# The TensorE work of a mixture-of-experts stage put into one written order, in a kernel that runs a chain of network blocks

## The chip, the core and the metric

The kernel runs on one core of one Trainium2 chip. The metric is the device time of one execution in microseconds (us). All arrays are float32 in HBM. TensorE (PE in the rows) multiplies, VectorE (DVE) and ScalarE (ACT) do the element work, GpSimd (POOL) a little of it, and SyncE (SP) issues nearly all loads.

## The reference, cut to what matters

The network is a chain of blocks on 256 tokens of width 1024. The part at issue is the feed-forward of the first block, a mixture of 32 experts of which each token takes 4:

```python
def expert_block(args):
    xb, e = args
    u = xb @ w_mlp1[e] + b_mlp1[e]                     # 1024 -> 2048
    x_glu = jnp.minimum(u[..., ::2], SWIGLU_LIMIT)
    x_lin = jnp.clip(u[..., 1::2], -SWIGLU_LIMIT, SWIGLU_LIMIT)
    a = x_glu * jax.nn.sigmoid(SWIGLU_ALPHA * x_glu) * (x_lin + 1)
    return a @ w_mlp2[e] + b_mlp2[e]                   # 1024 -> 1024
...
out = jnp.zeros((T + 1, D), jnp.float32).at[slot_tok].add(ys.astype(jnp.float32) * slot_gate[:, None])
```

One expert has 8 MiB of first weights and 4 MiB of second weights, so the 32 experts have 384 MiB, and each of them is read once.

## The kernel before

`moe` (L1944) takes the 32 experts in 16 pairs, `for p in range(16)` (L1980). The tokens of the two experts of a pair share the 128 columns that TensorE holds: 64 and 64 slots, or 96 and 32 slots in the four pairs after the first ("wide" pairs, `WIDE`). A product with a slice of 64 (or 32) slots uses only that part of the array, so products of different slices can run side by side.

The weights come as 384 loads of 1 MiB (`chunks`, L2057): for each pair 16 for the first product (8 steps of 128 rows, one load for each expert) and 8 for the second (4 double steps). They go round through 14 buffers of 1 MiB, nine of the pool `wm` and five of the pool `wp` (`chunk`, L2052). SyncE issues a load when its buffer has been read for the last time.

A pair has these parts, in the order in which the program writes them:

- `slots(p+1)`: VectorE writes the one-hot matrices `S` and `SG` of the next pair.
- `bias` (L2034): b_mlp1 added to the four accumulators `u` by products with one-hot rows, 8 instructions. In the first pair it follows `up`, in the others it goes ahead.
- `up` (L2154): 64 products of 128x512 (128 in a wide pair), for each step k, each quarter n, each expert.
- `hidden` (L2168): the activation, on VectorE and ScalarE, quarter by quarter, into `a`.
- `take` (L1873): 16 products for each half b of the tokens gather the next pair's tokens into two accumulators `taken`; `inputs` (L2141) copies them to `X`, four copies on VectorE and four on ScalarE.
- `give` (L2217): 4 products add the results of the previous pair to the output `y`.
- `shares` (L2180): two transposes of `SG`. `turned` (L2189): 8 transposes of `a`, copied to `aT` by ScalarE in two halves.
- `bias` with b_mlp2, 4 instructions, then `down` (L2199): 32 products of 128x512 (64 in a wide pair).
- `results` (L2211): ScalarE copies the two accumulators to `ye`.

The order that the program writes is not the order in which TensorE runs. A planner that knows the dependencies and has its own costs and due times orders each engine's instructions when the program is built, so products of one part may stand between those of another. `issue_after(ins)` binds an instruction to come behind another one on its engine. It adds no wait on a semaphore. Before the change only the loads of the first pair (`dma`, L127, `self.queue`) and the first pair's bias are bound so.

Accumulators of 128x512 lie in PSUM: four banks for `acc()` (the four of `u`) and four for `gps()`, which `taken`, `o`, the transposes and `give` share. A float32 product of 512 columns is two matmul records in the trace.

Of the kernel before, what the change touches and what calls it, by code (L numbers as in the profile page):

```python
# [18 lines left out]
P = 128  # L19
# [19 lines left out]
class Net:  # L39
    def __init__(self, ctx, tc, dram, cols):  # L40
        self.ctx, self.tc, self.nc, self.d, self.colat = ctx, tc, tc.nc, dram, cols
        self.n, self.normed, self.later, self.queue = 0, (), None, None
        e = ctx.enter_context
        self.cp = e(tc.tile_pool(name="cp", bufs=1))
        self.xp = e(tc.tile_pool(name="xp", bufs=1))
        self.sp = e(tc.tile_pool(name="sp", bufs=4))
        self.wp = e(tc.tile_pool(name="wp", bufs=5))
        self.psa = e(tc.tile_pool(name="psa", bufs=4, space=PSUM))
        self.psg = e(tc.tile_pool(name="psg", bufs=4, space=PSUM))
        self.cols = self.const("c_cols")  # L50
        self.ident = self.const("c_ident")
        self.mhalf = self.cp.tile([P, 1], F32, name="mhalf", tag="mhalf")
        self.nc.vector.memset(self.mhalf, -0.5)
        self.x = self.xp.tile([P, 2, D], F32, name="x", tag="x")
# [1818 lines left out]
    def take(self, banks, S, m, b):  # L1873

        for k in range(8):
            j = k % 4
            self.nc.tensor.matmul(  # L1877
                banks[k // 4][:, j * m : (j + 1) * m], self.x[:, b, k * P : (k + 1) * P], S[:, b, :m],
                start=b == 0 and j == 0, stop=b == 1 and j == 3,
            )  # L1880
# [63 lines left out]
    def moe(self, ctx, A2, B2, ahead):  # L1944


        nc, d = self.nc, self.d
        self.wm = self.pool(ctx, "wm", self.WM)
        self.turn = 0
        mp = self.pool(ctx, "moe")  # L1950
        y = self.tl(mp, [P, 2, D], "ymoe")
        bias = self.biases(mp)
        self.queue = []
        nc.gpsimd.memset(y, 0.0)
        hot4 = self.tl(mp, [P, 32], "id4")
        nc.vector.tensor_reduce(hot4, self.ident.rearrange("p (r e) -> p e r", r=4), axis=AX.X, op=ALU.add)
        QG, perm, ei = (self.Q, self.G), hot4, None

        def slots(p):

            wide = 0 < p <= self.WIDE
            S = self.tl(mp, [P, 2, P], "S", bufs=2) if p else None
            SG = self.tl(mp, [P, 2, P], "SG", bufs=2)
            hs = self.tl(mp, [P, P], "hot", F32R, bufs=2)
            ws, at = [], 0
            for h, n in enumerate((96, 32) if wide else (64, 64)):
                c = 2 * p + h
                q, g = ([QG[i][:, b, c : c + 1] for b in range(2)] for i in range(2))
                self.chosen(q, g, n, at, S, SG)
                nc.gpsimd.tensor_copy(hs[:, at : at + n], perm[:, c : c + 1].to_broadcast([P, n]))  # L1970

                step = 32 if wide else 64
                ws.append((c, [slice(i, i + step) for i in range(at, at + n, step)]))
                at += n
            return S, SG, hs, ws

        with self.tc.high_priority():
            X = self.inputs(mp, self.taken, P, A2, B2)
        now, give = slots(0), None
        for p in range(16):  # L1980
            _, SG, hs, ws = now
            w = [(d["w_mlp1"][c], d["w_mlp2"][c]) if p == 0 else self.weights(self.expert(ei[0:1, c : c + 1])) for c, _ in ws]
            loads = self.chunks([(*wc, sls) for wc, (_, sls) in zip(w, ws)], self.chunk)
            if p == 0:
                qg, perm, cnt, ei = self.pairs(mp)
                QG = qg[:, 0], qg[:, 1]
            if p < 15:
                now = slots(p + 1)
            u = [self.acc() for _ in range(4)]
            begin = lambda: self.bias(u, bias[0], hs, P, p > 0, p == 0)  # L1990
            last = self.up(u, X, loads, None if p == 0 else begin)
            if p == 0:
                with self.tc.issue_after(last):
                    begin()
            a = self.hidden(mp, u, P)
            if p < 15:
                taken = [self.gps() for _ in range(2)]
                for b in range(2):
                    self.take(taken, now[0], P, b)
                X = self.inputs(mp, taken, P, A2, B2)  # L2000
            if give:
                give()
            sT = self.shares(mp, SG, P)
            aT = self.turned(mp, a, P)
            o = [self.gps() for _ in range(2)]
            self.bias(o, bias[1], hs, P, True, False)
            self.down(o, aT, loads)
            if p == 15:
                ahead()
            give = self.results(mp, o, sT, y, P)  # L2010
            if p == 0:
                self.queue = None
                self.ada_row(self.g2)
                items = self.overflow_items(mp, cnt)
        give()
        with self.tc.issue_after(self.split_v):
            n = nc.values_load(
                items[0][0:1, 0:1], min_val=0, max_val=self.ITEMS, skip_runtime_bounds_check_because="computed on the chip"
            )
        self.overflow(mp, QG, ei, A2, B2, y, n, items)  # L2020
        return y
# [12 lines left out]
    def bias(self, banks, b, hot, m, first, last):  # L2034

        parts = (b.h, b.l)
        for j, part in enumerate(parts):
            for n, bank in enumerate(banks):
                r = slice(32 * n, 32 * n + 32)
                self.nc.tensor.matmul(  # L2040
                    bank[:m, :], hot[r, :m], part[r, :], start=first and j == 0, stop=last and j == len(parts) - 1
                )

    def expert(self, v, engines=(mybir.EngineType.SP,)):
        return self.nc.values_load(
# [57 lines left out]
    def overflow(self, mp, QG, ei, A2, B2, y, n, items):  # L2103
        nc, d = self.nc, self.d
        _, ci, bf = items
        with self.tc.For_i(0, n, 1) as i:
# [23 lines left out]
                self.take(taken, S, 64, b)  # L2130
            X = self.inputs(mp, taken, 64, A2, B2)
            u = [self.acc() for _ in range(4)]
            self.up(u, X, loads, lambda: begin(u, b1))
            sT = self.shares(mp, SG, 64)
            aT = self.turned(mp, self.hidden(mp, u, 64), 64)
            o = [self.gps() for _ in range(2)]
            begin(o, b2)
            self.down(o, aT, loads)
            self.results(mp, o, sT, y, 64)()

    def inputs(self, mp, taken, m, A2, B2):  # L2141
# [9 lines left out]
                    self.ts(X[:, k, :m], src, A2[:, k : k + 1], ALU.mult, B2[:, k : k + 1], ALU.add)  # L2151
        return X

    def up(self, u, X, loads, begin=None):  # L2154

        if begin:
            begin()
        for k in range(8):
            raws = next(loads)
            for n in range(4):  # L2160
                for raw, sl in raws:
                    last = self.nc.tensor.matmul(  # L2162
                        u[n][sl, :], X[:, k, sl], raw[:, n * 512 : (n + 1) * 512],
                        start=k == 0 and not begin, stop=k == 7 and bool(begin),
                    ).ins
        return last

    def hidden(self, mp, u, m):  # L2168
        a = self.tl(mp, [P, D], "a")
# [10 lines left out]
    def shares(self, mp, SG, m):  # L2180

        sT = self.tl(mp, [P, 2, P], "sT", bufs=2)
        ps = self.gps()
        for b in range(2):
            self.nc.tensor.transpose(ps[:m, b * P : (b + 1) * P], SG[:, b, :m], self.ident)
        self.nc.vector.tensor_copy(sT[:m], ps[:m, :T].rearrange("p (b t) -> p b t", b=2))
        return sT

    def turned(self, mp, a, m):  # L2189
        aT = self.tl(mp, [P, 8, P], "aT")  # L2190
        for q in range(2):
            ps = self.gps()
            for j in range(4):
                k = 4 * q + j
                self.nc.tensor.transpose(ps[:, j * m : (j + 1) * m], a[:m, k * P : (k + 1) * P], self.ident[:m, :m])
            self.nc.scalar.copy(aT[:, 4 * q : 4 * q + 4, :m], ps[:, : 4 * m].rearrange("p (k s) -> p k s", s=m))
        return aT

    def down(self, o, aT, loads):  # L2199

        for k in range(0, 8, 2):
            raws = next(loads)
            for f in range(2):
                for n in range(2):
                    for raw, sl in raws:
                        self.nc.tensor.matmul(  # L2206
                            o[n][sl, :], aT[:, k + f, sl], raw[:, f * D + n * 512 : f * D + (n + 1) * 512],
                            start=False, stop=k + f == 7,
                        )

    def results(self, mp, o, sT, y, m):  # L2211

        ye = self.tl(mp, [P, D], "ye")
# [3 lines left out]
        def give():  # L2217
            for b in range(2):
                for n in range(2):
                    s = slice(n * 512, (n + 1) * 512)  # L2220
                    ps = self.gps()
                    self.nc.tensor.matmul(ps, sT[:m, b, :], ye[:m, s], start=True, stop=True)  # L2222
                    self.tt(y[:, b, s], y[:, b, s], ps, ALU.add)

        return give
# [144 lines left out]
```

## Time and profile before

| | us |
|---|---|
| three runs | 2844.01, 2849.41, 2851.41 |
| median | 2849.41 |
| profiled execution, its own time | 2851.98 |
| its span, first to last instruction | 2850.2 |
| mean granted TensorE clock | 0.966 of full speed |

The page of the profile shows TensorE busy for 96% of the span, VectorE for 47%, ScalarE for 33%. The expert stage stands between about 184 and 1239 us of the span. A busy time of TensorE is the union of its records, so it doesn't tell how many products ran side by side. A wait is put down to what released it, and a line like "PE g L2206" names engine, tile and line.

### The profile page before, as it was taken

To read this page: it belongs to the slowest core of one execution; us is meant where nothing else is said; L and a number is where in the kernel's file an instruction comes from. 1 tells how busy PE (TensorE), PEld (TensorE's weight loads), DVE (VectorE), ACT (ScalarE), POOL (GpSimd) and SP (SyncE) were. 2 spreads that over 40 slices of the span, in tenths; PEclk is the share of its full clock that TensorE was granted. 3 is DMA by queue.
4 is the path that set the end of the run, shared out by engine and by line. 5 is a ranking of instruction groups with operands and counts; after the bars stand their busy time and mean duration, and the time that the engine had idled before them with its cause. 6 is when DMAs were issued, how large, how long until landed. Compare 5 with 4: busy or idle time off the path is not lost. (4 is left out here: it accounts for less than half of the span.)

```text
span 2850.2 us, 41585 instructions
## 1 busy us (share of the span) xinstructions
PE 2743.4 (96%) x16810; PEld 1937.4 (68%) x16810; DVE 1337.9 (47%) x2395; ACT 930.2 (33%) x1648; POOL 201.3 (7%) x242
## 2 busy tenths in 40 slices
PE   6999999999999999978999999999999999999998
PEld 4764333333433333358899899898889899886898
DVE  3542211211111111158598765566675565566754
ACT  4421000000001000046454454444464454444642
POOL 2120000000000000015000000100010100112100
PEclk8989999999999999989999999999999999999999
DMA  8868999999999999953274465455465375381551
GB/s 294 263 269 324 383 390 404 394 384 394 389 386 384 383 384 379 414 185 118 99 251 163 138 229 178 159 182 168 160 223 191 109 251 187 112 182 33 205 180 57
DMA packets 312456, 710.91 MB, mean 249 GB/s; under 512 B 41403, under 2 KB 218905, under 8 KB 277317
## 3 DMA queue, kind: packets, MB, share of 16 engines
q1 hardware_dynamic: 309509, 699.19, 67.4%
q0 software_dynamic: 2752, 9.03, 1.0%
q8 instruction: 133, 2.18, 0.3%
q14 instruction: 62, 0.51, 0.1%
HBM read 707.12 MB, written 1.05 MB: 248 GB/s over the span
## 5 line engine op out<-in xcount | busy, mean ns | idle before, releaser
L103 DVE TENSOR_TENSOR wl<-raw,wh 128x1024 fp32r<-128x1024 f32 (+1 forms) x501 | 607.1, 1223 | 329.5 <-ACT wh L118 327.0
L118 ACT CAST wh<-raw 128x1024 fp32r<-128x1024 f32 (+1 forms) x501 | 514.1, 1044 | 406.5 <-PE g L179 287.3
L178 PE MATMUL g<-xTh,wh 128*128 128x256 f32 (+1 forms) x2216 | 634.6, 286 | 3.2 <-ACT wh L118 2.4
L180 PE MATMUL g<-xTh,wl 128*128 128x256 f32 (+1 forms) x2216 | 630.0, 284 | 0.0
L179 PE MATMUL g<-xTl,wh 128*128 128x256 f32 (+1 forms) x2216 | 629.9, 284 | 0.0
L2162 PE MATMUL acc<-raw,X 128*64 128x512 f32 (+1 forms) x2560 | 517.6, 598 | 0.5 <-DVE X L109 0.5
L178 PEld LDWEIGHTS g<-xTh,wh 128*128 128x128 f32 (+1 forms) x2216 | 426.2, 192 | 14.3 <-ACT wh L118 4.9
L179 PEld LDWEIGHTS g<-xTl,wh 128*128 128x128 f32 (+1 forms) x2216 | 426.2, 192 | 4.7
L180 PEld LDWEIGHTS g<-xTh,wl 128*128 128x128 f32 (+1 forms) x2216 | 425.9, 192 | 1.6 <-DVE state L476 0.3
L2162 PEld LDWEIGHTS acc<-raw,X 128*64 128x64 f32 (+1 forms) x2560 | 184.7, 126 | 317.1 <-issue 315.4
L2206 PE MATMUL g<-raw,aT 128*64 128x512 f32 (+1 forms) x1280 | 302.7, 657 | 0.0
L178 PE MATMUL acc<-wh,hsh 128*128 128x512 f32 x536 | 212.8, 398 | 1.1 <-ACT hsh L118 1.1
L179 PE MATMUL acc<-wl,hsh 128*128 128x512 f32 x536 | 210.2, 393 | 0.0
L180 PE MATMUL acc<-wh,hsl 128*128 128x512 f32 x536 | 207.2, 391 | 0.0
L115 ACT ACTIVATE sg<-gl 128x256 f32<-128x256 f32 x64 | 26.6, 417 | 551.1 <-DVE gl L107 551.1
L2206 PEld LDWEIGHTS g<-raw,aT 128*64 128x64 f32 (+1 forms) x1280 | 87.8, 137 | 167.6 <-issue 156.4
L107 DVE TENSOR_SCALAR gl<-acc 128x256 f32<-128x256 f32 x64 | 26.8, 418 | 366.7 <-PE acc L2162 348.5
L178 PE MATMUL g<-wh,xTh 128*128 128x256 f32 (+1 forms) x488 | 145.8, 299 | 4.5 <-DVE xTl L112 4.1
L180 PE MATMUL g<-wh,xTl 128*128 128x256 f32 (+1 forms) x488 | 143.6, 294 | 6.1 <-DVE xTl L103 6.1
L179 PE MATMUL g<-wl,xTh 128*128 128x256 f32 (+1 forms) x488 | 142.1, 291 | 0.2 <-DVE r L107 0.2
L109 DVE TENSOR_SCALAR X<-g,A,B 128x128 f32<-128x128 f32 x64 | 21.9, 405 | 247.0 <-PE g L1877 247.0
L103 DVE TENSOR_TENSOR ymoe<-ymoe,g 128x512 f32<-128x512 f32 x64 | 43.9, 688 | 184.0 <-PE g L2222 183.9
(546 smaller groups left out, 3033.0 us busy)
## 6 DMA issues: line engine op xcount, KB each, us to landing
raw<-in_w_mlp_dram SPq DMA_DIRECT2D x384, 1024.0 KB, 9.8
raw<-in_l_ffn_w_in_dram SPq DMA_DIRECT2D x88, 1024.0 KB, 5.3
raw<-in_l_ffn_w_out_dram SPq DMA_DIRECT2D x44, 1024.0 KB, 5.0
raw<-in_l_gm_w_in_dram SPq DMA_DIRECT2D x24, 1024.0 KB, 5.3
raw<-in_ffn_w_up_dram SPq DMA_DIRECT2D x22, 1024.0 KB, 5.3
raw<-in_w_ada_dram SPq DMA_DIRECT2D x20, 1024.0 KB, 8.3
raw<-in_w_in_dram SPq DMA_DIRECT2D x15, 1024.0 KB, 9.3
raw<-in_l_gm_w_out_dram SPq DMA_DIRECT2D x12, 1024.0 KB, 5.0
```

Source lines behind the costliest of these rows:

```text
L103: return (eng or self.nc.vector).tensor_tensor(out, a, b, op=op).ins
L107: (eng or self.nc.vector).tensor_scalar(out, a, s1, None, op0=op0)
L109: (eng or self.nc.vector).tensor_scalar(out, a, s1, s2, op0=op0, op1=op1)
L115: return self.nc.scalar.activation(out, a, f, **kw).ins
L118: h = self.nc.scalar.copy(s.h, v).ins
L178: mm(out, a.h, b.h, start=start, stop=False)
L179: mm(out, a.h, b.l, start=False, stop=False)
L180: mm(out, a.l, b.h, start=False, stop=stop)
L2162: last = self.nc.tensor.matmul(u[n][sl, :], X[:, k, sl], raw[:, n * 512 : (n + 1) * 512], start=k == 0 and not begin, stop=k == 7 and bool ...
L2206: self.nc.tensor.matmul(o[n][sl, :], aT[:, k + f, sl], raw[:, f * D + n * 512 : f * D + (n + 1) * 512], start=False, stop=k + f == 7,)
```

## The change

All products of the expert stage go through a new helper `mm`, which binds each one behind the one before it (`mm_last`), so that TensorE runs them in the order in which the program writes them. The products of `pairs` and `ada_row` in the first pair are not bound. The written order itself changes: `give` of the previous pair stands behind the first step of `up`; the transposes of `SG` come right behind `up`; the next pair's `take` is in two halves, each followed by a half of the transposes of `a`; b_mlp2 comes behind `down` instead of ahead of it; b_mlp1 is one piece ahead of `up`. In `up` and `down` the loops are as they were, so the two experts alternate product by product.

```diff
         for k in range(8):
             j = k % 4
-            self.nc.tensor.matmul(
+            self.mm(
                 banks[k // 4][:, j * m : (j + 1) * m], self.x[:, b, k * P : (k + 1) * P], S[:, b, :m],
                 start=b == 0 and j == 0, stop=b == 1 and j == 3,
             )
...
-        now, give = slots(0), None
+        now, give, self.mm_last = slots(0), None, []
...
             begin = lambda: self.bias(u, bias[0], hs, P, p > 0, p == 0)
-            last = self.up(u, X, loads, None if p == 0 else begin)
+            if p:
+                begin()
+            self.up(u, X, loads, p > 0, give)
             if p == 0:
-                with self.tc.issue_after(last):
-                    begin()
+                begin()
             a = self.hidden(mp, u, P)
+            sT, aT = self.shares(mp, SG, P), self.tl(mp, [P, 8, P], "aT")
             if p < 15:
                 taken = [self.gps() for _ in range(2)]
-                for b in range(2):
-                    self.take(taken, now[0], P, b)
+            for q in range(2):
+                if p < 15:
+                    self.take(taken, now[0], P, q)
+                self.turn_half(aT, a, P, q)
+            if p < 15:
                 X = self.inputs(mp, taken, P, A2, B2)
-            if give:
-                give()
-            sT = self.shares(mp, SG, P)
-            aT = self.turned(mp, a, P)
             o = [self.gps() for _ in range(2)]
-            self.bias(o, bias[1], hs, P, True, False)
-            self.down(o, aT, loads)
+            self.down(o, aT, loads, False)
+            self.bias(o, bias[1], hs, P, False, True)
             if p == 15:
                 ahead()
...
+    def mm(self, *at, to=None, **how):
+
+        with ExitStack() as after:
+            for ins in self.mm_last or ():
+                after.enter_context(self.tc.issue_after(ins))
+            ins = (to or self.nc.tensor.matmul)(*at, **how).ins
+        if self.mm_last is not None:
+            self.mm_last = [ins]
...
-    def up(self, u, X, loads, begin=None):
-
-        if begin:
-            begin()
+    def up(self, u, X, loads, begun, between=None):
+
         for k in range(8):
             raws = next(loads)
             for n in range(4):
                 for raw, sl in raws:
-                    last = self.nc.tensor.matmul(
+                    self.mm(
                         u[n][sl, :], X[:, k, sl], raw[:, n * 512 : (n + 1) * 512],
-                        start=k == 0 and not begin, stop=k == 7 and bool(begin),
-                    ).ins
-        return last
+                        start=k == 0 and not begun, stop=k == 7 and begun,
+                    )
+            if k == 0 and between:
+                between()
```

`bias`, `shares`, `turn_half` (half of what `turned` did), `down` and `give` call `mm` in the same way. The loop for overflowing tokens, `overflow`, uses the same functions without binding.

## Rows read from the trace of the kernel before

**Rows 1.** Busy time by stage: the stretch in us, its length, then for each engine the busy us and the instructions (x), the granted TensorE clock, the busy share of the 16 DMA engines, and the GB/s that they moved.

```profile
143.00:199.00 56.00, 50.38 (x255) 38.41 (x253) 25.42 (x67) 13.84 (x38) 13.47 (x18) 0.80 0.74 283
199.00:256.00 57.00, 55.16 (x222) 23.34 (x224) 22.33 (x84) 8.30 (x18) 1.77 (x6) 0.93 0.79 312
256.00:288.00 32.00, 32.00 (x141) 12.19 (x140) 5.58 (x15) 3.85 (x8) 0.00 (x0) 1.00 0.75 294
288.00:542.00 254.00, 252.10 (x1763) 89.83 (x1758) 46.56 (x131) 21.66 (x48) 1.68 (x8) 0.95 0.98 396
542.00:1130.00 588.00, 583.74 (x2284) 231.18 (x2283) 104.22 (x289) 48.75 (x108) 3.74 (x18) 0.97 0.98 385
1130.00:1187.00 57.00, 56.52 (x224) 21.96 (x222) 8.60 (x21) 3.91 (x8) 0.00 (x0) 0.97 1.00 404
1187.00:1239.00 52.00, 49.76 (x198) 19.59 (x197) 8.25 (x21) 5.38 (x10) 0.00 (x0) 0.93 0.71 278
1239.00:1260.00 21.00, 7.88 (x31) 6.66 (x30) 13.33 (x27) 10.87 (x30) 7.34 (x14) 0.67 0.28 88
```

**Rows 2.** Who waited for whom between 200 and 1220 us: the engine (SPq is SyncE's queue, PEld TensorE's weight load) and line, what ended the wait, us in total, times, the longest.

```profile
SPq L132 <- PE acc L2162: 425.7, 245, 22.4
SPq L132 <- PE g L2206: 370.9, 81, 13.7
...
PEld acc L2162 <- DMA raw<-in_w_mlp_dram: 0.8, 1, 0.8
```

**Rows 3.** TensorE in order of time over one pair of 64 and 64 slots: start, length, operation, and how many records were merged (x). Two records are one float32 product.

```profile
673.18 0.38 PE L2185 MATMUL g<-c_ident,SG 128*128 128x128 f32 x2
673.49 26.70 PE L2162 MATMUL acc<-raw,X 128*64 128x512 f32 x112
700.12 0.74 PE L2040 MATMUL acc<-b_mlp1h,hot 32*128 32x512 f32 x2
...
704.86 0.49 PE L2040 MATMUL g<-b_mlp2l,hot 32*128 32x512 f32 x2
705.28 7.06 PE L2206 MATMUL g<-raw,aT 128*64 128x512 f32 x20
...
712.91 3.65 PE L2206 MATMUL g<-raw,aT 128*64 128x512 f32 x12
...
729.23 2.84 PE L2222 MATMUL g<-ye,sT 128*128 128x512 f32 x6
732.00 5.42 PE L2162 MATMUL acc<-raw,X 128*64 128x512 f32 x16
...
738.32 0.38 PE L2185 MATMUL g<-c_ident,SG 128*128 128x128 f32 x2
```

**Rows 4.** The same view for a wide pair (96 and 32 slots): its first record, a stretch of `down` read from 404.0 to 405.5 us, and the first record of the pair after it.

```profile
350.60 0.38 PE L2185 MATMUL g<-c_ident,SG 128*128 128x128 f32 x2
...
403.42 2.35 PE L2206 MATMUL g<-raw,aT 128*32 128x512 f32 x20
...
414.73 0.38 PE L2185 MATMUL g<-c_ident,SG 128*128 128x128 f32 x2
```

**Rows 5.** The same view for `down` of the pair before the last, its first records (read to 1166 us) and then those of 1167 to 1177 us, and for `down` of the last pair, whole.

```profile
1162.38 4.06 PE L2206 MATMUL g<-raw,aT 128*64 128x512 f32 x10
...
1166.70 10.52 PE L2206 MATMUL g<-raw,aT 128*64 128x512 f32 x48
...
1220.23 15.97 PE L2206 MATMUL g<-raw,aT 128*64 128x512 f32 x64
```

**Rows 6.** VectorE (first and last of the 16 instructions of one `hidden`) and ScalarE (the second `aT` copy) in order of time, and, from the page's costliest groups, VectorE's copies to `X` (busy us, mean ns of one, idle before).

```profile
698.50 0.42 DVE L107 TENSOR_SCALAR gl<-acc 128x256 f32<-128x256 f32 x1 [23.20 <-PE acc L2162]
...
703.69 0.43 DVE L103 TENSOR_TENSOR a<-ln,sg 128x256 f32<-128x256 f32 x1
...
704.96 0.59 ACT L2196 COPY aT<-g 128x512 f32<-128x512 f32 x1 [1.95 <-PE g L2195]
...
L109 DVE TENSOR_SCALAR X<-g,A,B 128x128 f32<-128x128 f32 x64 | 21.9, 405 | 247.0 <-PE g L1877 247.0
```

**Rows 7.** The view of Rows 1 for short stretches inside the pair of Rows 3: two of `up`, the first part of `down`, and its end with `give`.

```profile
684.00:692.00 8.00, 8.00 (x38) 3.26 (x37) 0.00 (x0) 0.00 (x0) 0.00 (x0) 1.00 1.03 412
692.00:700.00 8.00, 8.00 (x34) 2.90 (x30) 1.50 (x5) 0.74 (x2) 0.00 (x0) 1.00 1.04 418
...
705.00:709.00 4.00, 4.00 (x12) 1.22 (x14) 0.00 (x0) 0.55 (x1) 0.42 (x2) 0.57 1.00 412
...
722.00:732.00 10.00, 10.00 (x38) 3.46 (x34) 2.81 (x8) 2.68 (x6) 0.00 (x0) 1.00 0.89 349
```

**Rows 8.** DMA issues: the expert weights issued between 180 and 1240 us, and, from the page, loads of the same size in a later stage: issuing queue, how many (x), KB of each, median us from issue to landing.

```profile
raw<-in_w_mlp_dram SPq DMA_DIRECT2D x370, 1024.0 KB, 9.8
...
raw<-in_l_ffn_w_in_dram SPq DMA_DIRECT2D x88, 1024.0 KB, 5.3
```

**Rows 9.** TensorE in order of time: 16 records of a `take` ahead of the stage, the first records of `up` in the first pair, the start of its `down`, and the `give` behind it.

```profile
184.15 2.02 PE L1877 MATMUL g<-S,x 128*128 128x128 f32 x16 [1.00 <-DVE S L109]
...
198.96 3.39 PE L2162 MATMUL acc<-raw,X 128*64 128x512 f32 x6 [0.51 <-DVE X L109]
...
252.00 8.47 PE L2206 MATMUL g<-raw,aT 128*64 128x512 f32 x32
...
277.64 1.88 PE L2222 MATMUL g<-ye,sT 128*128 128x512 f32 x4
```

More of the change, by code (lines that the diff above doesn't have):

```diff
@@ L41, in __init__ @@
         self.ctx, self.tc, self.nc, self.d, self.colat = ctx, tc, tc.nc, dram, cols
-        self.n, self.normed, self.later, self.queue = 0, (), None, None
+        self.n, self.normed, self.later, self.queue, self.mm_last = 0, (), None, None, None
         e = ctx.enter_context
@@ L2015, in moe @@
         give()
+        self.mm_last = None
         with self.tc.issue_after(self.split_v):
@@ L2039, in bias @@
                 r = slice(32 * n, 32 * n + 32)
-                self.nc.tensor.matmul(
+                self.mm(
                     bank[:m, :], hot[r, :m], part[r, :], start=first and j == 0, stop=last and j == len(parts) - 1
                 )
+    def mm(self, *at, to=None, **how):
[5 more added lines that the diff above has]
+            self.mm_last = [ins]
     def expert(self, v, engines=(mybir.EngineType.SP,)):
@@ L2132, in overflow @@
             u = [self.acc() for _ in range(4)]
-            self.up(u, X, loads, lambda: begin(u, b1))
+            begin(u, b1)
+            self.up(u, X, loads, True)
             sT = self.shares(mp, SG, 64)
@@ L2137, in overflow @@
             begin(o, b2)
-            self.down(o, aT, loads)
+            self.down(o, aT, loads, True)
             self.results(mp, o, sT, y, 64)()
@@ L2161, in up @@
                 for raw, sl in raws:
-                    last = self.nc.tensor.matmul(
+                    self.mm(
                         u[n][sl, :], X[:, k, sl], raw[:, n * 512 : (n + 1) * 512],
-                        start=k == 0 and not begin, stop=k == 7 and bool(begin),
-                    ).ins
-        return last
+                        start=k == 0 and not begun, stop=k == 7 and begun,
+                    )
+            if k == 0 and between:
+                between()
     def hidden(self, mp, u, m):
@@ L2184, in shares @@
         for b in range(2):
-            self.nc.tensor.transpose(ps[:m, b * P : (b + 1) * P], SG[:, b, :m], self.ident)
+            self.mm(ps[:m, b * P : (b + 1) * P], SG[:, b, :m], self.ident, to=self.nc.tensor.transpose)
         self.nc.vector.tensor_copy(sT[:m], ps[:m, :T].rearrange("p (b t) -> p b t", b=2))
@@ L2191, in turned, with turn_half, down @@
         for q in range(2):
[L2192 to L2196, printed above, removed]
-        return aT
-    def down(self, o, aT, loads):
+            self.turn_half(aT, a, m, q)
+        return aT
+    def turn_half(self, aT, a, m, q):
+        ps = self.gps()
+        for j in range(4):
+            k = 4 * q + j
+            self.mm(
+                ps[:, j * m : (j + 1) * m], a[:m, k * P : (k + 1) * P], self.ident[:m, :m], to=self.nc.tensor.transpose
+            )
+        self.nc.scalar.copy(aT[:, 4 * q : 4 * q + 4, :m], ps[:, : 4 * m].rearrange("p (k s) -> p k s", s=m))
+    def down(self, o, aT, loads, begun):
         for k in range(0, 8, 2):
@@ L2205, in down @@
                     for raw, sl in raws:
-                        self.nc.tensor.matmul(
+                        self.mm(
                             o[n][sl, :], aT[:, k + f, sl], raw[:, f * D + n * 512 : f * D + (n + 1) * 512],
-                            start=False, stop=k + f == 7,
+                            start=k + f == 0 and not begun, stop=k + f == 7 and begun,
                         )
@@ L2221, in give @@
                     ps = self.gps()
-                    self.nc.tensor.matmul(ps, sT[:m, b, :], ye[:m, s], start=True, stop=True)
+                    self.mm(ps, sT[:m, b, :], ye[:m, s], start=True, stop=True)
                     self.tt(y[:, b, s], y[:, b, s], ps, ALU.add)
```

## The prediction, made before the changed kernel was run

> **What bounds the kernel now.** I read first the busy time by stage, then the waits, then TensorE in order of time, and last the loads. The stage's regular part runs from 288 to 1130 us. There TensorE has a record running nearly all the time, and the 16 DMA engines are at 98% as well, with 385 to 396 GB/s [rows 1]. Two resources look full, so the waits must tell which one paces. SyncE waits for products of `up` and `down` to give buffers back, some 800 us in all, while TensorE waits for a weight once, for 0.8 us [rows 2]. So the loads are ahead and TensorE sets the pace. But they are not far from being the bound themselves, and that caps whatever TensorE can win.
>
> TensorE's order of time shows where its pace goes. A pair of 64 and 64 slots lasts 738.32 - 673.18 = 65.1 us [rows 3], a wide one 414.73 - 350.60 = 64.1 us [rows 4]. In the steady part of a `down` that nothing interrupts, 48 records take 10.52 us, of which the last one's own length is about 0.59 (the two halves overlap). (10.52 - 0.59) / 23 = 0.43 us for two records side by side [rows 5]. In a wide pair 20 records take 2.35 us, (2.35 - 0.59) / 4 = 0.44 for four at a time [rows 4]. The float32 product is two records, so `up` has 128 records and could take 64 x 0.43 = 27.5 us, and `down` 64 records, 13.8. The trace shows more: `up` takes 5.4 us for its first step (16 records) and 26.6 for the other seven, 32.0 together; `down` starts at 705.28 and ends at 729.23 with the gathers of a later pair in between, and its first 20 records take 7.06 and a 12-record piece 3.65, 0.30 to 0.35 for each record instead of 0.215 [rows 3]. The reader is to see that TensorE is "busy" all along and yet half empty in places: wherever the piece of one expert begins or ends without its partner, one half of the array is idle.
>
> **The change, part by part.** *Alternation in `up`*: the ramp of the first step and the tail of the last go, 32.0 to 27.5, 4.5 us less. In the first step TensorE must have both experts' loads; as they come in turn from one queue, this costs at most one load, counted with the loads below.
>
> *`down` in one run*: 13.8 us. The first records run at half speed: 10 take 4.06 us [rows 5], and the clock between 705 and 709 us is 0.57 of full speed [rows 7], so at times the 1.2 GHz level and not 2.4; before it TensorE had run biases and transposes with idle time in between, 700.12 to 705.28 [rows 3]. Kept as it is, four steps of 0.85 instead of 0.43 add 1.7. If the gathers in the gap keep the clock up it is 0, if it lasts twice as long 3.4. I take 1.7.
>
> *The gap between `up` and `down`* is now 5.2 us [rows 3]. After the change it holds the transposes of `SG` (0.3), two `take` halves and 8 transposes of `a`. The trace has 16 records of a `take` in 2.02 us [rows 9]; a half is 16 records, so two are 4.0; the transposes are about 1.5 in all. TensorE's own work is thus 5.8, the lower bound. VectorE's activation runs over 698.50 to 704.12, ending 4 us after the last product [rows 3, 6], so it lies beside the gathers. Then `o` needs banks, of which there are four under `gps()`: the `X` copies must empty `taken` (4 x 0.405 = 1.6 on VectorE, as much on ScalarE) and ScalarE must copy `aT` (0.59) [rows 6]. Queued behind this wait is all of `down`, and behind that the release of 8 buffers. With nothing overlapping the upper bound is 4.0 + 4.0 + 1.5 + 1.6 + 0.6 = 12 us. I take 7, near the lower one, because the second half of `a` is due at 4 us and the second `take` ends at about 4.5, and because the bank of the first transposes is free early.
>
> *The biases.* b_mlp1 stood in the gap at no cost and now stands on the path: 8 instructions in two groups of four, 1.3 us by 0.74 for the first group [rows 3]. b_mlp2 behind `down` is 0.9 by 0.49 for two records, twice [rows 3]. `ye` waits for it, and `give` for `ye`; the first step of `up` (3.4 us) covers two copies of 0.6.
>
> *`give`*: moved, not cut, 8 records at 0.46: 3.7 us [rows 3]. VectorE's additions are beside `up`, which leaves it idle (23.20 us before the activation [rows 6]).
>
> Sum for TensorE in a pair: 27.5 + 3.7 + 7 + 13.8 + 1.7 + 0.9 + 1.3 = 55.9 us, 9 less than now. A wide pair has the same, as four records run at a time.
>
> *The loads then become the bound.* While they are not held up they run at 412 and 418 GB/s, and only where TensorE gives no buffers back do they fall, to 349 [rows 7]. One load is 1.0486 MB / 415 GB/s = 2.52 us, a pair's 24 are 60.5 us. That is above 55.9, so a pair can't go below 60.5: of the 9 us only some 4.6 stay in each pair once the 14 full buffers are used up. TensorE then waits some 4.6 us in each pair.
>
> The stage's end follows from the loads. 370 of the 384 are issued after 180 us [rows 8], the first of them when the first buffer is free, some 3.4 us after 198.96 [rows 9], landing 5 us later as an unloaded one does [rows 8]: 207. The other 369 take 369 x 2.52 = 930, up to 1137. In the first pair `up` gives 16 buffers back in 30 us, of which DMA fills 12, and in the long gap behind it (bias, activation, half clock, some 14 us) the four others are soon used up; I estimate 7 us of idle DMA, 1144. One last step of `down` (3.4) and b_mlp2 (0.9) give 1148. Check by TensorE: the first pair now spans 198.96 to 277.64 [rows 9] and would take some 60 without its interruptions, then 15 x 55.9 = 839: 1098, earlier than 1148, so the loads decide.
>
> `down` of the last pair now ends at 1220.23 + 15.97 = 1236.2 [rows 5]. The gain is 1236 - 1148 = 88 us. What follows (last `give`, the loop for overflow, the next block) moves along with it; the next block's first weights now come behind a full queue, for which I take off 4. The profiled execution has 2851.98 us: 2851.98 - 84 = 2768, and as it lies 2.6 above the median, **2766 us**.
>
> About the loads' rate the Trainium skill has a rule that speaks against the change. DMA: Bandwidth & Descriptors, section Specifications, gives about 358 GB/s as HBM's limit for one core and 435 as the ceiling of the fabric. By the first a pair's weights would take 70 us, no gain at all; the stretches of 412 and 418 GB/s disagree with it here and fit the second.
>
> **The rivals.**
>
> *TensorE still bounds.* The planner still orders VectorE and ScalarE. If the `X` copies or the additions to `ymoe` come ahead of the activation there, or banks come free late, the gap is 12 us, and if the clock loss doubles to 3.4, the pair takes 55.9 + 5 + 1.7 = 62.6: 199 + 65 + 15 x 62.6 = 1203, 33 us gained, about 2817. For it speaks that the order is now rigid, so nothing fills a wait; against it that VectorE has only 16 instructions in the gap.
>
> *No change: the loads don't get faster.* If the 385 GB/s of the regular part were what the DMA gives on average, 24 loads are 65.4 us, as now, and the time stays 2850. Its 98% busy share speaks for it [rows 1]; against it are the dips to 349 exactly where SyncE waits for `down`, and that the wait is for TensorE [rows 2, 7].
>
> *Slower: the clock.* TensorE now waits between steps, and where it worked loosely the clock was at the lower level for a time (0.57 in the gap; 0.80 from 143 to 199 us, busy 50.4 of 56) [rows 1, 7]. At 1.2 GHz a share f of the 41.3 us of `up` and `down` costs f x 41.3 more. Up to f = 11% the loads hide it (60.5 - 55.9 = 4.6); from (65.1 - 55.9) / 41.3 = 22% on the pair is slower than now. At half, a pair takes 76.5 and the kernel some 2851 + 15 x 11.5 = 3020. Against it: a slow TensorE stops waiting for loads and is then fully busy, and in such stretches the clock is 1.00 [rows 7].
>
> The Trainium skill states this danger: TensorE: Matmul & The Clock Gate, section Loop structure matters more than you think, has loads awaited between products as the bad loop, in which TensorE goes cold. By that rule each starved step would run at the lower level; no row of before has such a wait.
>
> **How the numbers follow.** Loads as the bound: 0.68, at 2748 to 2790 (no idle DMA in the first pair and 418 GB/s throughout give some 12 us less; a hole of DMA of 1 to 2 us in each pair gives up to 25 more). TensorE still bound, 2790 to 2840: 0.17. No change: 0.05. Slower by the clock: 0.08. The last 0.02 is for an order on another engine that costs more than the gap's upper bound. Within 0.3% (8.5 us) is what a measurement can't tell from nothing. A part of the second case, 0.02, falls there, so: faster 0.83, same 0.07, slower 0.10. The range reaches down to 2745 and into the second case, to 2828.
>
> **What would show it.** `up` in one run of 128 records, broken only by `give`, and `down` in one run of 64. TensorE's waits for expert loads rise from 0.8 to some 50 us (10 or 11 pairs of 4.6), and SyncE's waits for products fall. The regular part moves 410 GB/s or more, with a pair at 60.5 us and the first pairs below that. The gap is 6 to 8 us. Wrong would be: a gap above 11, a clock below 0.9 in the regular part, or a load rate that stays at 385 with SyncE no longer waiting.

## The result, and the profile after

The changed kernel takes 2764.06 us (median of four runs, 2760.25 to 2767.18), the one before 2849.77 (2844.01 to 2851.41): a ratio of 0.970, 95% interval 0.968 to 0.972. The profiled execution has 2766.88 us and a span of 2765.1, 85.1 less than before.

The first view is busy time by stage, with the columns of [rows 1].

```profile
199.00:256.00 57.00, 54.19 (x264) 21.35 (x265) 22.43 (x85) 9.74 (x21) 1.35 (x4) 0.99 0.89 360
...
288.00:542.00 254.00, 234.05 (x1766) 90.83 (x1760) 55.11 (x159) 25.18 (x58) 1.67 (x8) 0.99 1.02 416
542.00:1050.00 508.00, 458.73 (x2134) 187.32 (x2129) 95.65 (x264) 43.60 (x98) 3.73 (x18) 1.00 1.02 417
```

In the regular part the loads move 416 to 417 GB/s where they moved 385 to 396 [rows 1], and TensorE is now idle for a tenth of it (458.73 busy of 508). The kernel got faster while its busiest engine became less busy, which is what a handover of the bound looks like.

The waits between 200 and 1150 us, with the columns of [rows 2], say who waits for whom:

```profile
PE acc L2051 <- DMA raw<-in_w_mlp_dram: 72.8, 53, 2.6
...
PE g L2051 <- DMA raw<-in_w_mlp_dram: 10.0, 14, 1.4
...
SPq L132 <- DMA raw<-in_w_mlp_dram: 434.9, 252, 3.2
SPq L132 <- PE acc L2051: 144.7, 98, 25.6
SPq L132 <- PE g L2051: 83.6, 52, 9.0
```

TensorE's products wait 72.8 + 10.0 = 83 us for weights. Before they never did; only its weight loads had two short waits, of 0.8 us [rows 2] and of 0.3, which the prediction's "once" leaves out. SyncE waits 228 us for products instead of 797 [rows 2]. L2051 is the line of the helper `mm`, so from here on products are told apart by their tiles.

TensorE in order of time over one pair of 64 and 64 slots answers to [rows 3]. The 16 records of a half of `take` are 8 products of two records each, and not 16 products:

```profile
645.22 0.44 PE L2051 MATMUL g<-c_ident,SG 128*128 128x128 f32 x2
645.49 1.95 PE L2051 MATMUL g<-S,x 128*128 128x128 f32 x16
647.28 0.60 PE L2051 MATMUL g<-c_ident,a 128*128 128x128 f32 x4
647.72 1.95 PE L2051 MATMUL g<-S,x 128*128 128x128 f32 x16
649.50 0.60 PE L2051 MATMUL g<-c_ident,a 128*128 128x128 f32 x4
650.03 11.37 PE L2051 MATMUL g<-raw,aT 128*64 128x512 f32 x50
...
665.79 0.50 PE L2051 MATMUL g<-b_mlp2h,hot 32*128 32x512 f32 x2
665.81 0.50 PE L2051 MATMUL acc<-b_mlp1h,hot 32*128 32x512 f32 x2
...
666.92 3.92 PE L2051 MATMUL acc<-raw,X 128*64 128x512 f32 x16
670.78 3.70 PE L2051 MATMUL g<-ye,sT 128*128 128x512 f32 x8
...
687.11 3.65 PE L2051 MATMUL acc<-raw,X 128*64 128x512 f32 x16 [1.32 <-DMA raw<-in_w_mlp_dram]
692.07 3.65 PE L2051 MATMUL acc<-raw,X 128*64 128x512 f32 x16 [1.31 <-DMA raw<-in_w_mlp_dram]
...
705.61 0.44 PE L2051 MATMUL g<-c_ident,SG 128*128 128x128 f32 x2
```

The pair lasts 705.61 - 645.22 = 60.4 us. The gap between `up` and `down` is 645.22 to 650.03, 4.8 us without one idle stretch. The late steps of `up` start 692.07 - 687.11 = 4.96 us apart though TensorE needs 3.65, the rest is the wait for two more loads. The transposes of `a` don't wait either: the last piece of `a` is written at 708.83 + 0.42 in the next pair, 0.65 before its transposes begin at 709.90, and the copies to `X` follow at once.

```profile
708.83 0.42 DVE L103 TENSOR_TENSOR a<-ln,sg 128x256 f32<-128x256 f32 x1
709.21 1.37 DVE L109 TENSOR_SCALAR X<-g,A,B 128x128 f32<-128x128 f32 x4
```

A wide pair early in the stage, while full buffers are still in store, shows what TensorE needs without any wait, 340.99 - 289.57 = 51.4 us:

```profile
289.57 0.44 PE L2051 MATMUL g<-c_ident,SG 128*128 128x128 f32 x2
...
294.38 13.94 PE L2051 MATMUL g<-raw,aT 128*32 128x512 f32 x128
...
309.38 3.64 PE L2051 MATMUL acc<-raw,X 128*32 128x512 f32 x32
312.95 3.70 PE L2051 MATMUL g<-ye,sT 128*128 128x512 f32 x8
...
340.99 0.44 PE L2051 MATMUL g<-c_ident,SG 128*128 128x128 f32 x2
```

`up` is interrupted by `give` from 312.95 to 316.58 only, 28.0 us without it. Of the 9 us between 51.4 and 60.4, the trace of the pair at 645.22 calls some 6.1 idle (0.81 in `down` and four waits of 1.31 to 1.34 in `up`). The rest counts as busy.

And at the end of the stage, the last piece of `down` and the first product of the next block:

```profile
1148.02 3.65 PE L2051 MATMUL g<-raw,aT 128*64 128x512 f32 x14 [1.41 <-DMA raw<-in_w_mlp_dram]
...
1166.58 1.97 PE L240 MATMUL g<-c_ident,z 128*128 128x128 f32 x8 [9.89 <-DVE z L107]
```

In the kernel before, that product of the next block stands here:

```profile
1252.44 1.97 PE L240 MATMUL g<-c_ident,z 128*128 128x128 f32 x8 [12.62 <-DVE z L107]
```

`down` of the last pair ends at 1151.7 instead of 1236.2 [rows 5], 84.5 us earlier. That is all but 0.6 of the 85.1 us: the gain arises in the expert stage and stays.

### The profile page after: what moved, and what is told of

Read it like the earlier page. It is cut to its first block, busy times and chain, and to the rows that moved or that the text cites. A ratio compares the mean times of both kernels' runs of the same rounds, so it can differ in the third digit from the quotient of the medians.

```text
span 2765.1 us, 41516 instructions
## 1 busy us (share of the span) xinstructions
PE 2581.7 (93%) x16801; PEld 1883.9 (68%) x16810; DVE 1337.3 (48%) x2395; ACT 928.0 (34%) x1648; POOL 202.5 (7%) x242
## 5 line engine op out<-in xcount | busy, mean ns | idle before, releaser
L2051 PE MATMUL acc<-raw,X 128*64 128x512 f32 (+1 forms) x2560 | 479.6, 599 | 73.3 <-DMA raw<-in_w_mlp_dram 72.8
L2051 PEld LDWEIGHTS acc<-raw,X 128*64 128x64 f32 (+1 forms) x2560 | 156.5, 126 | 384.0 <-issue 233.8
L2051 PE MATMUL g<-raw,aT 128*64 128x512 f32 (+1 forms) x1280 | 237.5, 595 | 9.8 <-DMA raw<-in_w_mlp_dram 9.8
L2051 PEld LDWEIGHTS g<-raw,aT 128*64 128x64 f32 (+1 forms) x1280 | 80.1, 126 | 155.5 <-issue 124.2
L180 PEld LDWEIGHTS acc<-wh,hsl 128*128 128x128 f32 x536 | 100.6, 188 | 22.3 <-DVE hsl L103 0.3
## 6 DMA issues: line engine op xcount, KB each, us to landing
raw<-in_w_mlp_dram SPq DMA_DIRECT2D x384, 1024.0 KB, 19.8
```

Of the source, the lines that this page charges most:

```text
L180: mm(out, a.l, b.h, start=False, stop=stop)
L2051: ins = (to or self.nc.tensor.matmul)(*at, **how).ins
```

## The experiments

The theory: after the change the loads set the pace of the stage, 60.4 us in a pair, TensorE needs 51.4 and has 9 us to spare. Whatever costs TensorE less than 9 us a pair is free, more is paid in full, and fewer bytes are time won. The rivals: TensorE is still on the path; or the order, and not its sum of work, is what counts. Each kernel was timed beside the kernel before on the same chip, and ratios are to that one.

**The new order without the binding.**

```diff
-        now, give, self.mm_last = slots(0), None, []
+        now, give, self.mm_last = slots(0), None, None
```

> The changed kernel with its new written order, but no product bound behind another. Theory (the binding does it, because the planner otherwise goes back to blocks of one expert and puts gathers into the second product): TensorE's pair stays near 65 us against 60.4 for the loads, and the time is 2830 to 2855. Rival (the new written order does it and the binding adds nothing): 2764, with a pair of 60.4 us.

Measured: 2850.4 us, ratio 1.000 (0.999 to 1.001). The planner put the gathers of a later pair into `up` and the experts back into blocks:

```profile
737.16 5.42 PE L2051 MATMUL acc<-raw,X 128*64 128x512 f32 x16
742.51 3.17 PE L2051 MATMUL g<-S,x 128*128 128x128 f32 x26
745.61 5.42 PE L2051 MATMUL acc<-raw,X 128*64 128x512 f32 x16
...
751.83 19.61 PE L2051 MATMUL acc<-raw,X 128*64 128x512 f32 x80
...
802.08 5.42 PE L2051 MATMUL acc<-raw,X 128*64 128x512 f32 x16
```

A step of 16 records takes 5.42 us again, as in [rows 3], and the pair 802.08 - 737.16 = 64.9. So the way the parts are written is worth nothing by itself; the binding is what makes it the order of the chip.

**The binding with the old order of the parts.**

```diff
-            self.up(u, X, loads, p > 0, give)
+            self.up(u, X, loads, p > 0)
...
-            sT, aT = self.shares(mp, SG, P), self.tl(mp, [P, 8, P], "aT")
             if p < 15:
                 taken = [self.gps() for _ in range(2)]
-            for q in range(2):
-                if p < 15:
-                    self.take(taken, now[0], P, q)
-                self.turn_half(aT, a, P, q)
-            if p < 15:
+                for b in range(2):
+                    self.take(taken, now[0], P, b)
                 X = self.inputs(mp, taken, P, A2, B2)
+            if give:
+                give()
+            sT = self.shares(mp, SG, P)
+            aT = self.turned(mp, a, P)
             o = [self.gps() for _ in range(2)]
-            self.down(o, aT, loads, False)
-            self.bias(o, bias[1], hs, P, False, True)
+            self.bias(o, bias[1], hs, P, True, False)
+            self.down(o, aT, loads, True)
```

> All products bound, but the parts in the order in which the kernel before wrote them: both gathers, then the previous results, then all transposes, the second bias ahead of the second product. Theory (the loads are the bound, any order with a TensorE pair under 60.4 us is as good): the gap grows by the 3.6 us of the results, which leave the first product in exchange; the pair needs about 52 us of TensorE, and the time is 2764 within 5. Rival (the halves beside the activation are needed): the pair needs over 60.4 us and the time is 2785 or more.

Measured: 2768.1 us, ratio 0.971 (0.969 to 0.973).

```profile
706.69 3.84 PE L2051 MATMUL g<-S,x 128*128 128x128 f32 x32
710.36 3.60 PE L2051 MATMUL g<-ye,sT 128*128 128x512 f32 x8
...
714.02 1.04 PE L2051 MATMUL g<-c_ident,a 128*128 128x128 f32 x8
...
715.94 13.95 PE L2051 MATMUL g<-raw,aT 128*64 128x512 f32 x64
```

The gap is 715.94 - 706.69 = 9.25 us, but `give` lies in it and no longer in `up`, and the last 8 transposes run without a wait because `a` is ready by then. In the regular part a pair is 60.2 to 61.3 us. The halves beside the activation are not needed for the gain. The binding is what this kernel has and the one before, in the same order, has not.

**Experts in blocks, all else as changed.** In `up` and `down` the loops over the quarters n and the experts change places.

```diff
-            for n in range(4):
-                for raw, sl in raws:
+            for n, (raw, sl) in by_expert(raws, 4):
+                if True:
...
+def by_expert(raws, parts):
+    order = []
+    for raw in dict.fromkeys(id(r) for r, _ in raws):
+        order += [(n, rs) for n in range(parts) for rs in raws if id(rs[0]) == raw]
+    return order
```

> The changed kernel with the experts in blocks: in each step all quarters of one expert, then all of the other, still bound and with the new order of the parts. Theory (the loads are the bound): the first product goes back from 27.5 to 32 us, the second loses some 2 us, TensorE needs about 58 us in a pair, less than 60.4, and the time is 2764 to 2772. Rival (alternation is what the gain needs; the second product goes back to 19.6 us too): 62 us in a pair, 2785 to 2790.

Measured: 2769.6 us, ratio 0.971 (0.970 to 0.973). With loads in store a pair takes 56.3 us, 5 more than with alternation, then 60.3 to 61.0. Alternation is worth 5 us of TensorE's work in a pair, and here these 5 us buy nothing that the intervals tell from noise. In the steady part TensorE looks full again:

```profile
542.00:1000.00 458.00, 456.89 (x1912) 188.97 (x1909) 85.04 (x235) 37.53 (x86) 3.33 (x16) 1.00 1.02 417
```

456.89 busy of 458, yet the loads (417 GB/s) set the pace, as in the changed kernel. What shows is the length of the same records: seven steps of `up`, 112 records, took 26.70 us in the kernel before [rows 3]; here, read to 770 us, 109 of them take 28.56, without an idle stretch between them.

```profile
732.69 5.42 PE L2051 MATMUL acc<-raw,X 128*64 128x512 f32 x16
...
741.67 28.56 PE L2051 MATMUL acc<-raw,X 128*64 128x512 f32 x109
```

In that run some records start alone, 0.43 us apart, from 761.26 to 762.55 for instance, where elsewhere two start within 0.06. One half of the array works there, presumably while the other half's load is awaited, and that counts as busy.

**Slack measured by added work.** The gather is done once more, and then four times more, into the same banks (the last one counts). The edit is the first kernel's; the second has `range(8)`.

```diff
                 taken = [self.gps() for _ in range(2)]
+                for i in range(2):
+                    self.take(taken, now[0], P, i % 2)
             for q in range(2):
```

> The changed kernel with the gather of the next pair's tokens done twice (the first result is overwritten), which adds 2 x 1.8 = 3.6 us of TensorE work to the gap of each of 15 pairs. Theory (TensorE has 9 us to spare in a pair): same time as the changed kernel, 2764 within 5, and its waits for expert loads fall by about 50 us. Rival (TensorE is still on the path): 15 x 3.6 = 54 us more, 2818.

> The changed kernel with the gather done five times instead of once: 4 x 3.6 = 14.3 us more TensorE work in each of 15 pairs. Theory (9 us to spare): TensorE then needs 51.4 + 14.3 = 65.7 us in a pair and is the bound again, as before the change; 199 + 59 + 14 in the first pair + 15 x 65.7 puts the end of the last products near 1245 against 1152, and the time near 2855. Rival (the work is hidden by the waits altogether): 2764.

Measured: with one more gather 2761.9 us, ratio 0.969 (0.968 to 0.971), and TensorE's products wait 55 us for expert loads instead of 83. The waits were expected to fall by about 50 and fell by 28. Half-empty steps, which count as busy, would explain the difference; that was not tried by itself. With four more 2851.9 us, ratio 1.0005 (0.9993 to 1.0018): the kernel before once more, by another way. Its pair is 759.95 - 694.43 = 65.5 us, and SyncE is back to waiting for products, 398.5 and 357.5 us between 200 and 1250 us:

```profile
694.43 0.44 PE L2053 MATMUL g<-c_ident,SG 128*128 128x128 f32 x2
...
759.95 0.44 PE L2053 MATMUL g<-c_ident,SG 128*128 128x128 f32 x2
```

3.6 us a pair cost nothing, 14.3 cost 5.1 in each pair: 65.5 - 60.4. Between them lies the 9 us of slack.

**Fewer bytes, in the changed kernel and in the one before.** Each load of the second weights brings half, used for both steps.

```diff
-                    self.dma(
-                        raw.rearrange("p (f n) -> p f n", f=2), w2[r : r + 2 * P, :].rearrange("(f p) n -> p f n", p=P)
-                    )
+                    self.dma(raw[:, :D], w2[r : r + P, :])
...
-                            o[n][sl, :], aT[:, k + f, sl], raw[:, f * D + n * 512 : f * D + (n + 1) * 512],
+                            o[n][sl, :], aT[:, k + f, sl], raw[:, n * 512 : (n + 1) * 512],
```

> The changed kernel with half of the second weights left out: each of the 8 loads of a pair's second product is 0.5 MiB and is used for both steps (a wrong result; 20 instead of 24 MiB in a pair). Theory (the loads are the bound): a pair's loads take 50.3 us, TensorE needs 51.4 and takes over; the last products end near 199 + 59 + 15 x 51.4 = 1029 against 1152, and the time is about 2645, surely below 2680. Rival (something else holds the pair at 60 us): 2764.

> The same half of the second weights left out of the kernel before (a wrong result). Theory (there TensorE is the bound, not the loads): same time as before, 2850 within 9. Rival (DMA at 98% was a second bound in it): up to 15 x 4 = 60 us less, below 2830.

Measured: in the changed kernel 2639.6 us, ratio 0.926 (0.924 to 0.928), 124 us less than with all loads. Its pairs are 749.13 - 697.91 = 51.2 us, TensorE's own need, and between 300 and 1000 us SyncE waits for products alone (311.7 and 199.5 us) and no longer for an earlier load:

```profile
697.91 0.44 PE L2051 MATMUL g<-c_ident,SG 128*128 128x128 f32 x2
...
749.13 0.44 PE L2051 MATMUL g<-c_ident,SG 128*128 128x128 f32 x2
```

In the kernel before the same cut gives 2841.0 us, ratio 0.997 (0.996 to 0.998).

```profile
542.00:1000.00 458.00, 454.70 (x1814) 178.76 (x1816) 85.03 (x240) 39.42 (x88) 2.92 (x14) 0.95 0.82 326
```

DMA falls to 326 GB/s and 82% busy, and TensorE stays full: the loads did not bound the kernel before, in spite of their 98%. The 9.5 us are just outside what was expected. The steady pairs give only a part of them: 64.8 us against 65.1, 0.3 in each of some ten. The planner also ordered the products of the first two and the last two pairs otherwise, and the next block starts 2.6 us sooner after the last `down`. How the 9.5 us divide among these was not tried.

**What keeps the clock up in the gap.** The gathers go behind `down`.

```diff
-            if p < 15:
-                taken = [self.gps() for _ in range(2)]
             for q in range(2):
-                if p < 15:
-                    self.take(taken, now[0], P, q)
                 self.turn_half(aT, a, P, q)
-            if p < 15:
-                X = self.inputs(mp, taken, P, A2, B2)
             o = [self.gps() for _ in range(2)]
             self.down(o, aT, loads, False)
             self.bias(o, bias[1], hs, P, False, True)
+            if p < 15:
+                taken = [self.gps() for _ in range(2)]
+                for q in range(2):
+                    self.take(taken, now[0], P, q)
+                X = self.inputs(mp, taken, P, A2, B2)
```

> The changed kernel with both halves of the gather taken out of the gap and put behind the second product and its bias; all products stay bound. The gap then holds the transposes alone and waits for the activation, and the copies to X stand on the path ahead of the next first product. Theory (what keeps the clock at its upper level through the gap is the gathers in it): the clock falls to the 1.2 GHz level for some us at the start of the second product in most pairs, as in the kernel before, and TensorE needs 51.3 + about 4 us of waiting + 2 us for the copies + 2 to 3 us of slow clock, near 60, about what the loads take; time 2764 to 2785. Rival (the binding or the alternation keeps the clock up): no such fall, 2764.

Measured: 2764.3 us, ratio 0.9705 (0.969 to 0.972). The gap then holds transposes that wait for the activation, and `down` behind it can start slowly, as in [rows 7]:

```profile
301.86 0.44 PE L2050 MATMUL g<-c_ident,a 128*128 128x128 f32 x2 [1.14 <-DVE a L103]
```

```profile
302.00:310.00 8.00, 8.00 (x62) 2.28 (x65) 0.46 (x3) 0.59 (x1) 0.00 (x0) 0.79 1.02 426
```

The clock is 0.79 of full speed over the first 8 us of `down`; in the changed kernel the 8 us from 294 have 1.00.

```profile
294.00:302.00 8.00, 8.00 (x77) 2.58 (x78) 2.10 (x9) 1.99 (x5) 0.00 (x0) 1.00 1.03 422
```

Unhindered pairs take 55.9 to 57.0 us, 5 more than with the gathers in the gap, and still less than the loads.

The fall does not come in every pair. Over the first 6 us of `down` the granted clock lies between 0.54 and 0.80 in 9 of the 16 pairs and at 1.00 in the other 7, whose transposes waited just as long (0.6 and 1.1 us for the last two pieces of `a`). One of the 7, with 50 records in 11.37 us as in the changed kernel, is

```profile
713.88 11.37 PE L2050 MATMUL g<-raw,aT 128*64 128x512 f32 x50
```

In the changed kernel and with the old order bound it is 1.00 in all 16, in the kernel before 0.55 to 0.81 in 15 of 16. So with gathers in the gap the clock stayed at the upper level (2.4 GHz) every time, and binding and alternation by themselves don't keep it there. Whether the gathers do it as products or by taking up the wait was not told apart, and why 7 pairs were spared stays open. In this kernel it makes no difference to the time.

**Fewer microseconds for the same bytes.** If the loads are the bound, the way they are cut must matter. The second weights came as two pieces of 4 KB in each partition; here a partition takes two neighbouring rows in one piece of 8 KB, and the transposes of `a` take every second column to match.

```diff
-                        raw.rearrange("p (f n) -> p f n", f=2), w2[r : r + 2 * P, :].rearrange("(f p) n -> p f n", p=P)
+                        raw, w2[r : r + 2 * P, :].rearrange("(p f) n -> p (f n)", f=2)
...
+            two = a[:m, k // 2 * 2 * P : (k // 2 + 1) * 2 * P].rearrange("p (i f) -> p i f", f=2)
             self.mm(
-                ps[:, j * m : (j + 1) * m], a[:m, k * P : (k + 1) * P], self.ident[:m, :m], to=self.nc.tensor.transpose
+                ps[:, j * m : (j + 1) * m], two[:, :, k % 2], self.ident[:m, :m], to=self.nc.tensor.transpose
```

> The changed kernel with the second weights loaded as two neighbouring rows in one partition, 8 KB in one piece instead of two pieces of 4 KB; the transposes of the activation take every second column to match. Theory (the loads are the bound and the second weights land every 2.55 us instead of the 2.49 of the first ones): 128 loads x 0.06 us = 7.5 us less, 2756. Rival (the size of the pieces makes no difference): 2764; or the strided transposes cost TensorE time, which the waits hide.

Measured: 2756.2 us, ratio 0.967 (0.966 to 0.969). The intervals of this ratio and of the changed kernel's overlap, so both were run again side by side, five rounds each.

> The changed kernel itself, beside the next run on the same chip, so that the two can be compared: 2764 within 4.

> The changed kernel with the second weights in pieces of 8 KB, once more and beside the changed kernel. Theory (the second weights land 0.06 us apart faster each, 128 of them): 7 to 8 us less than the changed kernel. Rival (the difference seen before lies between chips): the same as the changed kernel within 3 us.

Measured: 2765.0 us (0.970, 0.968 to 0.972) and 2758.4 us (0.967, 0.966 to 0.969), 6.6 apart, after 7.8 the first time. The regular part, first of the changed kernel, then with long pieces:

```profile
542.00:1000.00 458.00, 411.20 (x1910) 166.13 (x1907) 84.84 (x235) 38.32 (x86) 3.33 (x16) 1.00 1.02 417
```

```profile
542.00:1000.00 458.00, 414.46 (x1924) 164.50 (x1920) 84.97 (x235) 38.33 (x86) 3.33 (x16) 1.00 1.01 420
```

417 becomes 420 GB/s; the whole stage's loads, 966 us at 417, take 7 less at 420. The landings in the two traces put it where it was expected: the second weights land 2.55 us apart in the changed kernel (mean of 40) and 2.49 to 2.50 with long pieces, the first ones 2.49 in both. The intervals still overlap, so the size of this gain is less sure than its direction, which two comparisons and the rate agree on. It is the fastest of the kernels here that do all the work.

## Why the prediction was right, point by point

**Which resource would bound: right, and shown from three sides.** Added TensorE work is free up to a slack that lies between 3.6 and 14.3 us a pair, fewer bytes win 124 us after the change and almost nothing before it, and a better cut of the same bytes wins 7. The step from "DMA 98% busy" to "not the bound yet" rested on the waits, and the cut of loads in the kernel before confirms it.

**The time of a load and the pace of a pair: right.** 2.52 us and 60.5 us were forecast, 60.4 was measured, at 416 to 417 GB/s. The Trainium skill (DMA: Bandwidth & Descriptors, section Specifications) states about 358 GB/s as HBM's limit for one core; the loads moved 416 to 417 here, and the measurement decides.

**TensorE's need: right in kind, too large by 4.5 us.** 55.9 was forecast, 51.4 measured.

| term | forecast us | measured us |
|---|---|---|
| `up` | 27.5 | 28.0 |
| `give` | 3.7 | 3.6 |
| gap | 7 | 4.8 |
| `down` | 13.8 | 13.9 |
| slow clock at its start | 1.7 | 0 |
| both biases | 2.2 | 1.1 |

The gap is even below the lower bound. Two gathers take 3.6 us and not 4.0, the row of [rows 9] having its last record's own length in it. The transposes of `a` take 1.0 and not 1.5, a figure for which the prediction shows no row. The wait for banks and for the second half of `a`, for which the 7 us allowed, didn't come. The second bias of one pair runs beside the first bias of the next (665.79 and 665.81), so the two take 1.1 us together where the prediction added them up. None of it reached the time, because the loads hide it.

**What followed from that term.** With 9 us to spare in a pair instead of 4.6, of which some 6 show as idle, TensorE waits 83 us instead of 50, and the buffers in store last for two pairs, not five.

**The stage's end: near, by two errors that cancel.** The last products were forecast to end at 1148 and end at 1151.7, 3.7 late. The loads of the first 57 us of the stage move 360 GB/s, (416 - 360) / 416 x 57 = 7.7 us lost, close to the 7 that were set aside. The allowance of 4 us for the next block wasn't needed: it starts 14.9 us after the last `down` where it was 16.2. So a forecast gain of 84 us met 85.1 partly by luck. By its own terms (2768, less 2.6) the last step also gives 2765 and not 2766, which changes nothing.

**The rivals.** TensorE as the bound at a gap of 12 us: the gap is 4.8, and the kernel with four more gathers shows what this rival would have looked like. No change, with 385 GB/s as DMA's limit: refuted by 417. Slower by the clock: the waits of 1.3 us in `up` did not bring the clock down, it is 0.99 to 1.00 over the regular part. What this rival meant does show in two pairs, where the last step of `up` waited longer for its load and then took 5.34 us instead of 3.65:

```profile
520.98 5.34 PE L2051 MATMUL acc<-raw,X 128*64 128x512 f32 x14 [2.58 <-DMA raw<-in_w_mlp_dram]
...
763.57 5.34 PE L2051 MATMUL acc<-raw,X 128*64 128x512 f32 x14 [2.44 <-DMA raw<-in_w_mlp_dram]
```

The clock is 0.72 from 520 to 526 us and 0.86 from 760 to 772. The Trainium skill's rule on awaited loads (TensorE: Matmul & The Clock Gate, section Loop structure matters more than you think) agrees with these two steps, and not with the many steps that waited 1.3 us at full clock. Both pairs take 63.2 us and the ones behind them 58.6, so most of the loss came back.

## What to carry to other kernels

When two resources are both near full, read who waits for whom, and then work out the second one's floor before the first one is improved: here it left 4.7 of the 14 us that TensorE won in a pair, and made the time easy to forecast. Where a planner orders an engine, write down the order only if you also bind it. After a change of bound, tune the new one (the cut of the loads) and leave the old one alone, for even the loss of alternation now costs nothing that the runs tell from noise.

## What the runs showed of the hardware that was not expected

- A half-empty array looks busy. Experts in blocks show 456.89 of 458 us busy, alternating ones 411.20, at the same pace. TensorE's busy time rises as products lose their partners.
- Blocks of one expert overlap by half. With experts in blocks, bound, a step alone takes 5.42 us for 16 records, as it does in the kernel before [rows 3]. One after the other they would need 16 x 0.43 = 6.9 us, alternating they take 3.65. Twelve times 0.43 is 5.2, so the first half of the second block runs beside the second half of the first, although four products of the first expert were issued ahead of it. In seven steps on end (26.70 us for 112 records [rows 3], 0.24 for each) only the first and the last half block run alone. This is why blocks cost 5 us a pair and not the 41 that one expert after the other would.
- SyncE now waits 435 us for earlier loads to land, which it did not do before, and a load lands 19.8 us after its issue (median of the page; 9.8 before). By these figures some 8 loads are on their way at once (an estimate, 19.8 / 2.52), where there were 4, and with 8 the loads move no more bytes than the 412 to 418 GB/s that they reached in [rows 7].
- With gathers, products of 128x128, in the gap, TensorE's clock is 1.00 at the start of all 16 `down` (changed, and old order bound). Where the gap has transposes that wait for the activation, it lies at 0.81 or less in 15 of 16 in the kernel before, in 15 of 16 unbound (0.58 to 0.79) and in 9 of 16 with the gathers behind.
